# Three 256-column matmuls per weight tile, into one PSUM accumulator, in a two-layer encoder trunk

## The chip, the cores and the metric

The kernel runs on one core of a Trainium2 chip. The time is device time in microseconds, the median of several executions. The engines are named as in the profile: PE is TensorE (PEld its loads of stationary tiles), DVE is VectorE, ACT is ScalarE, POOL is GpSimd, SP the engine that issues most DMAs.

## The reference

An encoder trunk of two layers, 256 tokens of 2048 features, all in float32:

```python
for i in range(DEPTH):                       # DEPTH = 2
    a = rms_norm(h, mix_norm[i])
    if i % N_MIXERS == 0:
        mixed = neighborhood_attention(a, na_w_qkv[j], na_rpb[j], na_w_o[j])   # layer 0
    elif i % N_MIXERS == 1:
        mixed = short_conv_mixer(a, sc_w_in[j], sc_conv_w[j], sc_w_out[j])     # layer 1
    h = h + mixed
    h = h + conv_glu_ffn(rms_norm(h, ffn_norm[i]), ffn_w_up[i], ffn_conv_w[i],
                         ffn_conv_b[i], ffn_w_down[i])
return rms_norm(h, final_norm)
```

Almost all of the work is in the products with the weights: 2048 x 6144 and 2048 x 2048 in each mixer, 2048 x 11264 and 5632 x 2048 in each gated MLP.

## The kernel before

Everything is kept transposed: features on the 128 partitions, the 256 tokens on the free axis. A weight tile of 128 x 128 is stationary, the activations of one feature tile move. float32 is carried in two parts of the type float32r: a weight w as wh + wl, an input x as xh + xl. Of the four products three are taken, wh*xh + wh*xl + wl*xh. An input tile (`a`, `act`) holds xh in its columns 0 to 255 and xl in 256 to 511.

The **weight stream** is two lists made ahead: `chunks`, the weights in order of first use (8 tiles of 128 x 128 as a rule, 512 KB), and `items`, TensorE's work. `prep_to` keeps the preparation four chunks ahead: a DMA on SP's queue to `raw` (L94), a copy by ACT to `hi` (L95), a subtraction by DVE to `lo` (L96). `Phase` makes the items of one product: an output tile of 128 features is a sum over `nk` weight tiles (16, or 22 for the second product of the MLP). `Phase.run` issues the matmuls, L134 and L135 for each weight tile. L134 multiplies wh with all 512 columns, xh and xl side by side, into a full PSUM bank: wh*xh lands in the lower half, wh*xl in the upper. L135 multiplies wl with xh, 256 columns, and adds into the upper half. So the lower half holds the main product, the upper the corrections. Four such accumulators (`mm`) are in turn.

When an output tile is complete, its **evacuation** adds the halves. After products that take a norm's input, `normed` copies the upper half to SBUF (L176, ACT), adds the lower (L177, DVE) and multiplies by the norm's factor rstd (L178, DVE). After products that end a branch, `residual` adds both halves to the stream hT (L211, L212, DVE). Then follow the convolutions, the gate, the next input's split in two parts, or the squares for the next norm (POOL, L219 and L220).

The **order** around it: layer 0 is queries and keys with the scores of two heads (`scores`, L265 to L267) and the values with the mix (`Values`, L328 to L330, and `mix`, L302 to L304) spread between the items by `after`, then the product with wo, then the MLP in two halves. Layer 1 is the product with wsc, the short convolution, the product with wscout, the MLP. At the start the inputs arrive while the first three output tiles are computed in turns over four weight tiles; their evacuation waits until rstd is known (`first_stats`: L205 sums the squares, L194 to L199 make rstd, L457 brings it to the other layout). Engines take their instructions in order; a scheduler fixes that order when the program is built, and it may place a small matmul such as L205 between the matmuls of other items.

`scores` and `mix` have products in three parts as well, each as three matmuls of 256 columns into one place:

```python
nc.tensor.matmul(o[:, i, :], lhsT=vh, rhs=p[:, :S], start=k == 0, stop=False)
nc.tensor.matmul(o[:, i, :], lhsT=vh, rhs=p[:, S:], start=False, stop=False)
nc.tensor.matmul(o[:, i, :], lhsT=vl, rhs=p[:, :S], start=False, stop=k == 1)
```

Of the kernel before, what the change touches and what calls it, by code (L numbers as in the profile page):

```python
"""Two-layer hybrid encoder trunk, kept transposed on chip: features on partitions, tokens on the
free axis. Weight tiles are stationary. A float32 product is carried by float32r parts:
w = wh + wl and x = xh + xl exactly, with 12 significant bits each, and
w*x = wh*xh + (wh*xl + wl*xh) to float32's rounding, so three passes give what four would.
"""
# [7 lines left out]
F32 = mybir.dt.float32  # L13
# [6 lines left out]
P = 128  # L20
D = 2048
S = 256
# [6 lines left out]
EPS = 1e-6  # L29
# [4 lines left out]

# columns of the packed parameters
C_NORM = 0
# [9 lines left out]
def trunk(ctx, tc, xT, par, bias, wqk, wv, wo, wsc, wscout, wup, wdown, out):  # L46
    nc = tc.nc
# [8 lines left out]
    hT = cp.tile([P, KT, S], F32, name="hT")  # L56
# [12 lines left out]
    nc.scalar.dma_start(out=pt[:, :C_SC], in_=par[:, :C_SC])  # L69
    # the activation table and TensorE's clock, while the first loads are under way  # L70
    nc.scalar.copy(out=tp.tile([P, 1], F32, name="m", tag="m"), in_=ones[:, :1])
# [10 lines left out]

# [1 line left out]
    items = []      # PE work, in order  # L84
    chunks = []     # weights, in order of first use
    prepped = []
# [12 lines left out]
    class Phase:  # L99
        """fts output tiles, each a sum over nk tiles of src, ended by evac(ft, psum)."""  # L100

# [24 lines left out]
        def run(self, ft, c, k0, ka, kb):  # L126
            hi, lo = prepped[c]
            if ka == 0:
                self.ps[ft] = pm.tile([P, 2 * S], F32, name="mm", tag="mm")
            ps = self.ps[ft]  # L130
            for k in range(ka, kb):
                x = self.src[k]
                o = (k - k0) * P
                nc.tensor.matmul(ps, lhsT=hi[:, o:o + P], rhs=x, start=k == 0, stop=False)  # L134
                nc.tensor.matmul(ps[:, S:], lhsT=lo[:, o:o + P], rhs=x[:, :S], start=False,  # L135
                                 stop=k == self.nk - 1)
            if kb == self.nk:
                held.append((self, ft))
                if not waiting:
                    evacuate()  # L140
# [7 lines left out]

    later = []      # (item number, function)

# [4 lines left out]

# [1 line left out]
    def split(dst, src):  # L157
        """src (float32) into its two float32r parts."""
        nc.scalar.copy(out=dst[:, :S], in_=src)
        nc.vector.tensor_sub(out=dst[:, S:], in0=src, in1=dst[:, :S].bitcast(F32))  # L160
# [12 lines left out]
    def normed(dst, ps):  # L173
        """dst = (both parts of a product of un-normalised input) * rstd."""
        corr = tp.tile([P, S], F32, name="corr", tag="corr", bufs=3)
        nc.scalar.copy(out=corr, in_=ps[:, S:])  # L176
        nc.vector.tensor_add(out=corr, in0=ps[:, :S], in1=corr)  # L177
        nc.vector.tensor_mul(out=dst, in0=corr, in1=rstd)  # L178

    def conv(x, w, b):  # L180
        """Centred three-tap convolution along the tokens of a zero-padded tile."""
        c = tp.tile([P, S], F32, name="conv", tag="conv", bufs=4)
        if b is None:
            nc.scalar.activation(c, x[:, 1:S + 1], AF.Copy, scale=w[1])
        else:
            nc.scalar.activation(c, x[:, 1:S + 1], AF.Identity, scale=w[1], bias=b)  # L186
        for tap in (0, 2):
            nc.vector.scalar_tensor_tensor(out=c, in0=x[:, tap:tap + S], scalar=w[tap], in1=c,  # L188
                                           op0=ALU.mult, op1=ALU.add)
        return c  # L190

    def rsqrt(dst, v, r, t, sums):
        """dst = (sums / D + EPS) ** -0.5, with a Newton step after the table's square root."""
        nc.vector.tensor_scalar(out=v, in0=sums, scalar1=1.0 / D, scalar2=EPS, op0=ALU.mult, op1=ALU.add)  # L194
        nc.scalar.activation(r, v, AF.Sqrt)
        nc.vector.reciprocal(out=r, in_=r)
        nc.vector.tensor_mul(out=t, in0=r, in1=r)
        nc.vector.scalar_tensor_tensor(out=t, in0=t, scalar=-0.5, in1=v, op0=ALU.mult, op1=ALU.mult)
        nc.vector.scalar_tensor_tensor(out=dst, in0=t, scalar=1.5, in1=r, op0=ALU.add, op1=ALU.mult)  # L199

    def stats(sums):
        """rstd of every token, on all partitions, from sums of squares."""
        ps = pa.tile([P, S], F32, name="st", tag="st")
        for i, x in enumerate(sums):
            nc.tensor.matmul(ps, lhsT=ones, rhs=x, start=i == 0, stop=i == len(sums) - 1)  # L205
        v = tp.tile([P, S], F32, name="v", tag="v", bufs=1)
        rt = tp.tile([P, 2, S], F32, name="rt", tag="s")
        rsqrt(rstd, v, rt[:, 0, :], rt[:, 1, :], ps)

    def residual(ps, ft):  # L210
        nc.vector.tensor_add(out=hT[:, ft, :], in0=ps[:, S:], in1=hT[:, ft, :])  # L211
        nc.vector.tensor_add(out=hT[:, ft, :], in0=ps[:, :S], in1=hT[:, ft, :])  # L212

# [8 lines left out]
    def to_norm(n, a):  # L222
        """Evacuation of a branch's output: residual, squares, and the next norm's input."""
        def evac(ft, ps):
            residual(ps, ft)
            a[ft] = a_tile()
            scaled_split(a[ft], hT[:, ft, :], norm_g(n, ft))
            squares(ft)
            if ft == KT - 1:
                after(1, lambda: stats([acc]))  # L230
        return evac

# [1 line left out]
    a0 = [None] * KT  # L234
# [49 lines left out]
    def probs(h):  # L284
        """The probabilities with keys on partitions: per key tile, both parts of (128, 256 queries)."""
        x = heads[h]
        tr = pa.tile([P, 2, S], F32, name="tr", tag="tr")
        for k in range(2):
            for t in range(2):
                nc.tensor.transpose(tr[:, k, t * P:(t + 1) * P], x["p"][:, t, k * P:(k + 1) * P], ident)  # L290
        x["pT"] = [act_tile(), act_tile()]
        for k in range(2):
            split(x["pT"][k], tr[:, k, :])

    def mix(hs, v):
        """Two heads' values, weighted by their probabilities."""
        o = pa.tile([P, 2, S], F32, name="o", tag="o")
        for i, h in enumerate(hs):
            for k in range(2):
                p = heads[h]["pT"][k]  # L300
                vh, vl = (x[:, h % 4 * P:(h % 4 + 1) * P] for x in v[k])
# [3 lines that stand above are left out]
        for i, h in enumerate(hs):  # L305
            oT[h] = act_tile()
            split(oT[h], o[:, i, :])
            heads[h].clear()

    class Values:  # L310
        """The values of four heads, tokens on partitions: the input is stationary."""

# [30 lines left out]

# [1 line left out]
    yT = [None] * KT  # L345
# [18 lines left out]

# [1 line left out]
    glu = {}  # L366
# [22 lines left out]

# [1 line left out]
    def last_evac(ft, ps):  # L391
        residual(ps, ft)
        if ft < KT - 1:
            squares(ft)
            nc.scalar.activation(hT[:, ft, :], hT[:, ft, :], AF.Copy, scale=norm_g(4, ft))
            if ft == 0:
                # brings in the table that the last norm needs
                nc.scalar.activation(tp.tile([P, 1], F32, name="m", tag="m"), ones[:, :1], AF.Sqrt)
            return
        q = tp.tile([P, S], F32, name="q", tag="q")  # L400
        nc.vector.tensor_mul(out=q, in0=hT[:, ft, :], in1=hT[:, ft, :])
        nc.vector.tensor_scalar_mul(hT[:, ft, :], hT[:, ft, :], norm_g(4, ft))
        # rstd with tokens on partitions, then spread over the partitions by a product with a diagonal
        col = pa.tile([P, 2], F32, name="o", tag="o")
# [30 lines left out]

# [1 line left out]
    sq = []  # L437
# [37 lines left out]
def _tiles(w, cols):  # L475
    """(K, N) -> (tiles of 128 columns in the order of cols, 128 rows of a K tile, K tiles * 128)."""
    import numpy as np
    k, n = w.shape
    t = np.asarray(w).reshape(k // P, P, n // P, P).transpose(2, 1, 0, 3)
    return np.ascontiguousarray(t[cols]).reshape(len(cols), P, k)  # L480
# [61 lines left out]
```

## Time and profile before

| | |
|---|---|
| median of 3 runs | 2264.58 us (2258.64 to 2269.03) |
| span of the profiled execution | 2279.6 us |
| PE busy | 2256.4 us, 99%, 12716 matmuls and as many loads |
| DVE busy | 1638.7 us, 72% |
| ACT busy | 1148.1 us, 50% |
| POOL busy | 178.1 us, 8% |
| DMA | 421.10 MB, mean 185 GB/s |
| mean granted TensorE clock | 0.994 of full speed |

The profiled execution has only its span as its own time; it is 15.0 us over the median of the runs. A group's line has the source line, the engine, the operation, output and inputs by the program's names, the shape of out and in, the count, then busy time, the mean of one in ns, and the engine's idle time just ahead with what ended most of it. Durations of matmuls overlap, since the engine is a pipeline: the distance between two starts says what one costs. Counts of matmuls on the profile can be above the program's where a float32 product takes two passes.

### The profile page before, as it was taken

What the parts mean: (1) busy time and instruction counts of PE and PEld (TensorE: products, weight loads), DVE (VectorE), ACT (ScalarE), POOL (GpSimd) and SP (SyncE); (2) the same over time, 40 slices, a digit from 0 to 9 for tenths busy, and PEclk for the clock granted to TensorE, in tenths of its full rate; (3) what the DMA queues carried; (4) which work ended last, traced back from release to release, by engine and by line L of the source; (5) the groups of instructions that cost most, each with busy time, mean ns of one, the idle gap of its engine ahead of it and who ended that gap; (6) DMA issues with size and microseconds to landing.
All of it is one profiled execution on the core that took longest, in us unless ns stands there. A gap on an engine that the chain in (4) does not pass through costs nothing.

```text
span 2279.6 us, 33316 instructions
## 1 busy us (share of the span) xinstructions
PE 2256.4 (99%) x12716; PEld 1955.2 (86%) x12716; DVE 1638.7 (72%) x2408; ACT 1148.1 (50%) x1694; POOL 178.1 (8%) x174
## 2 busy tenths in 40 slices
PE   8999999999999999999999999999999999999997
PEld 7888888888888888888888888888888888888886
DVE  8777668877775577776676666777777557777754
ACT  6555554555543455554444444455555334555542
POOL 3011003100000000001210000330000000000021
PEclk8999999999999999999999999999999999999998
DMA  7565555555556655556655555555555665555563
GB/s 241 189 187 177 178 173 191 183 187 187 187 175 189 193 189 188 186 181 182 189 188 185 186 188 188 186 185 185 186 186 183 181 190 192 186 187 187 175 189 104
DMA packets 119841, 421.10 MB, mean 185 GB/s; under 512 B 13568, under 2 KB 13568, under 8 KB 119680
## 3 DMA queue, kind: packets, MB, share of 16 engines
q1 hardware_dynamic: 117936, 414.72, 57.0%
q0 software_dynamic: 1024, 3.15, 0.5%
q8 instruction: 100, 1.64, 0.3%
q10 hardware_dynamic: 720, 1.09, 0.1%
q14 instruction: 61, 0.50, 0.1%
HBM read 416.81 MB, written 2.10 MB: 184 GB/s over the span
## 4 chain that ended last, share of the span: by engine, by line
PE 97%; DVE 1%; issue 0%; DMA 0%; POOL 0%; ACT 0%; SPq 0%; DVEq 0%; ACTq 0%
PE mm L134 61%; PE mm L135 31%; PE mm L328 1%; PE mm L329 1%; PE mm L330 1%; DMA hT<-in_xT 0%; DVE lo L96 0%; PE tr L290 0%; DVE hT L416 0%; PE st L205 0%; POOL acc L220 0%; PE o L302 0%; PE o L304 0%; PE o L303 0%; PE sc L266 0%
## 5 line engine op out<-in xcount | busy, mean ns | idle before, releaser
L134 PE MATMUL mm<-a,hi 128*128 128x512 f32 x4096 | 1454.4, 400 | 1.8 <-ACT hi L95 1.4
L96 DVE TENSOR_TENSOR lo<-raw,hi 128x1024 fp32r<-128x1024 f32 (+2 forms) x806 | 979.1, 1215 | 544.2 <-ACT hi L95 540.6
L95 ACT CAST hi<-raw 128x1024 fp32r<-128x1024 f32 (+2 forms) x806 | 827.2, 1027 | 1012.6 <-issue 599.2
L135 PE MATMUL mm<-a,lo 128*128 128x256 f32 x4096 | 1153.5, 282 | 5.2 <-DVE lo L96 5.2
L134 PEld LDWEIGHTS mm<-a,hi 128*128 128x128 f32 x4096 | 771.7, 188 | 193.1 <-ACT hi L95 1.7
L135 PEld LDWEIGHTS mm<-a,lo 128*128 128x128 f32 x4096 | 775.6, 189 | 7.3 <-DVE lo L96 6.9
L134 PE MATMUL mm<-act,hi 128*128 128x512 f32 x1920 | 675.6, 397 | 0.0
L135 PE MATMUL mm<-act,lo 128*128 128x256 f32 x1920 | 537.9, 280 | 0.0
L134 PEld LDWEIGHTS mm<-act,hi 128*128 128x128 f32 x1920 | 360.4, 188 | 87.9 <-DVE act L160 0.3
L135 PEld LDWEIGHTS mm<-act,lo 128*128 128x128 f32 x1920 | 362.4, 189 | 0.1
L188 DVE SCALAR_TENSOR_TENSOR conv<-pad,pt,conv 128x256 f32<-128x256 f32 x384 | 185.1, 482 | 11.1 <-ACT conv L186 4.3
L216 POOL TENSOR_TENSOR acc<-hT 128x256 f32<-128x256 f32 x4 | 3.4, 853 | 1599.2 <-DVE hT L212 1599.2
L186 ACT ACTIVATE conv<-pad,pt 128x256 f32<-128x256 f32 x176 | 105.2, 598 | 6.9 <-DVE pad L178 6.9
L177 DVE TENSOR_TENSOR corr<-mm,corr 128x256 f32<-128x256 f32 x256 | 106.8, 417 | 1.0 <-ACT corr L176 0.8
L176 ACT COPY corr<-mm 128x256 f32<-128x256 f32 x256 | 92.9, 363 | 0.9 <-PE mm L135 0.8
L219 POOL TENSOR_TENSOR q<-hT 128x256 f32<-128x256 f32 x59 | 70.6, 1196 | 242.1 <-DVE hT L212 242.1
L178 DVE TENSOR_TENSOR pad<-corr,rstd 128x256 f32<-128x256 f32 x176 | 75.1, 427 | 5.9
L211 DVE TENSOR_TENSOR hT<-mm,hT 128x256 f32<-128x256 f32 x96 | 40.2, 422 | 30.1 <-PE mm L135 30.0
L220 POOL TENSOR_TENSOR acc<-acc,q 128x256 f32<-128x256 f32 x59 | 59.8, 1014 | 4.6
L164 DVE SCALAR_TENSOR_TENSOR a<-hT,pt,a 128x256 fp32r<-128x256 f32 x64 | 55.5, 878 | 4.8 <-ACT a L163 4.8
L328 PE MATMUL mm<-hi,a 128*128 128x512 f32 x128 | 50.7, 396 | 0.0
L329 PE MATMUL mm<-lo,a 128*128 128x512 f32 x128 | 49.9, 390 | 0.0
(95 smaller groups left out, 762.0 us busy)
## 6 DMA issues: line engine op xcount, KB each, us to landing
raw<-in_wup SPq DMA_DIRECT2D x352, 512.0 KB, 3.7
raw<-in_wdown SPq DMA_DIRECT2D x128, 512.0 KB, 3.7
raw<-in_wsc SPq DMA_DIRECT2D x96, 512.0 KB, 3.6
raw<-in_wqk SPq DMA_DIRECT2D x58, 512.0 KB, 3.7
raw<-in_wdown SPq DMA_DIRECT2D x64, 384.0 KB, 3.2
raw<-in_wv SPq DMA_DIRECT2D x32, 512.0 KB, 3.8
raw<-in_wo SPq DMA_DIRECT2D x32, 512.0 KB, 3.6
raw<-in_wscout SPq DMA_DIRECT2D x32, 512.0 KB, 3.6
```

The costliest lines, as they stand in the source:

```text
L95: nc.scalar.copy(out=hi[:, :w], in_=raw[:, :w])
L96: nc.vector.tensor_sub(out=lo[:, :w], in0=raw[:, :w], in1=hi[:, :w].bitcast(F32))
L134: nc.tensor.matmul(ps, lhsT=hi[:, o:o + P], rhs=x, start=k == 0, stop=False)
L135: nc.tensor.matmul(ps[:, S:], lhsT=lo[:, o:o + P], rhs=x[:, :S], start=False, stop=k == self.nk - 1)
L176: nc.scalar.copy(out=corr, in_=ps[:, S:])
L177: nc.vector.tensor_add(out=corr, in0=ps[:, :S], in1=corr)
L178: nc.vector.tensor_mul(out=dst, in0=corr, in1=rstd)
L186: nc.scalar.activation(c, x[:, 1:S + 1], AF.Identity, scale=w[1], bias=b)
L188: nc.vector.scalar_tensor_tensor(out=c, in0=x[:, tap:tap + S], scalar=w[tap], in1=c, op0=ALU.mult, op1=ALU.add)
L219: nc.gpsimd.tensor_mul(out=q, in0=hT[:, ft, :], in1=hT[:, ft, :])
L328: nc.tensor.matmul(self.ps[t], lhsT=xh, rhs=wh, start=k == 0, stop=False)
L329: nc.tensor.matmul(self.ps[t], lhsT=xh, rhs=wl, start=False, stop=False)
```

## The change

The accumulator of an output tile becomes 256 columns, half a bank. For each weight tile there are three matmuls of 256 columns, all into it: wh with xh, wh with xl, wl with xh. `normed` is one multiplication from PSUM, `residual` one addition.

```diff
         def run(self, ft, c, k0, ka, kb):
             hi, lo = prepped[c]
             if ka == 0:
-                self.ps[ft] = pm.tile([P, 2 * S], F32, name="mm", tag="mm")
+                self.ps[ft] = pm.tile([P, S], F32, name="mm", tag="mm")
             ps = self.ps[ft]
             for k in range(ka, kb):
                 x = self.src[k]
-                o = (k - k0) * P
-                nc.tensor.matmul(ps, lhsT=hi[:, o:o + P], rhs=x, start=k == 0, stop=False)
-                nc.tensor.matmul(ps[:, S:], lhsT=lo[:, o:o + P], rhs=x[:, :S], start=False,
-                                 stop=k == self.nk - 1)
+                wh, wl = (w[:, (k - k0) * P:(k - k0 + 1) * P] for w in (hi, lo))
+                nc.tensor.matmul(ps, lhsT=wh, rhs=x[:, :S], start=k == 0, stop=False)
+                nc.tensor.matmul(ps, lhsT=wh, rhs=x[:, S:], start=False, stop=False)
+                nc.tensor.matmul(ps, lhsT=wl, rhs=x[:, :S], start=False, stop=k == self.nk - 1)
...
     def normed(dst, ps):
-        corr = tp.tile([P, S], F32, name="corr", tag="corr", bufs=3)
-        nc.scalar.copy(out=corr, in_=ps[:, S:])
-        nc.vector.tensor_add(out=corr, in0=ps[:, :S], in1=corr)
-        nc.vector.tensor_mul(out=dst, in0=corr, in1=rstd)
+        nc.vector.tensor_mul(out=dst, in0=ps, in1=rstd)
...
     def residual(ps, ft):
-        nc.vector.tensor_add(out=hT[:, ft, :], in0=ps[:, S:], in1=hT[:, ft, :])
-        nc.vector.tensor_add(out=hT[:, ft, :], in0=ps[:, :S], in1=hT[:, ft, :])
+        nc.vector.tensor_add(out=hT[:, ft, :], in0=ps, in1=hT[:, ft, :])
```

Lines below `Phase.run` have other numbers after the change: the three matmuls are L134, L135 and L136, the multiplication of `normed` is L175, the addition of `residual` L208, the statistics L202, the product that brings rstd to the other layout L453.

The order of instructions on TensorE, in the first up product of layer 0, at the boundary between two output tiles (numbers tell one buffer from the next; `mm` is the accumulator, `a` an input tile, `hi` and `lo` the parts of a weight chunk). Before:

```order
L134 MATMUL mm_8720<-a_4021,hi_8626 128x512
L135 MATMUL mm_8720<-a_4021,lo_8627 128x256
L134 MATMUL mm_8720<-a_4074,hi_8626 128x512
L135 MATMUL mm_8720<-a_4074,lo_8627 128x256
L134 MATMUL mm_8775<-a_3318,hi_8658 128x512
L135 MATMUL mm_8775<-a_3318,lo_8659 128x256
```

and with the change:

```order
L134 MATMUL mm_10544<-a_4730,hi_10432 128x256
L135 MATMUL mm_10544<-a_4730,hi_10432 128x256
L136 MATMUL mm_10544<-a_4730,lo_10433 128x256
L134 MATMUL mm_10612<-a_3761,hi_10469 128x256
L135 MATMUL mm_10612<-a_3761,hi_10469 128x256
L136 MATMUL mm_10612<-a_3761,lo_10470 128x256
```

Each pair has become three; nothing else stands between them. On DVE at the same output tile, the evacuation between the splits of weights, before:

```order
L177 TENSOR_TENSOR corr_8759<-mm_8720,corr_8759 128x256
L178 TENSOR_TENSOR pad0_78<-corr_8759,rstd_76 128x256
L96 TENSOR_TENSOR lo_8828<-raw_8826,hi_8827 128x1024
L188 SCALAR_TENSOR_TENSOR conv_8763<-pad0_78,pt_73,conv_8763 128x256 x2
L96 TENSOR_TENSOR lo_8851<-raw_8849,hi_8850 128x1024
L177 TENSOR_TENSOR corr_8814<-mm_8775,corr_8814 128x256
```

and with the change:

```order
L175 TENSOR_TENSOR pad0_78<-mm_10544,rstd_76 128x256
L96 TENSOR_TENSOR lo_10639<-raw_10637,hi_10638 128x1024
L185 SCALAR_TENSOR_TENSOR conv_10600<-pad0_78,pt_73,conv_10600 128x256 x2
L96 TENSOR_TENSOR lo_10678<-raw_10676,hi_10677 128x1024
L175 TENSOR_TENSOR pad1_79<-mm_10612,rstd_76 128x256
```

The addition to `corr` is gone, the rest of the order is kept. At the start of the program, on TensorE, the place of the last two of the four statistics matmuls (`st`) among the first three output tiles (`mm_226`, `mm_235`, `mm_244`), before:

```order
L134 MATMUL mm_235<-a_184,hi_218 128x512
L135 MATMUL mm_235<-a_184,lo_219 128x256
L205 MATMUL st_376<-act_178,ones_75 128x256
L134 MATMUL mm_244<-a_166,hi_262 128x512
L205 MATMUL st_376<-act_178,ones_75 128x256
L135 MATMUL mm_244<-a_166,lo_263 128x256
```

and with the change, where the last one comes behind the whole of the third tile (`mm_252`), and the product with rstd behind the whole of the fourth (`mm_468`):

```order
L135 MATMUL mm_252<-a_214,hi_332 128x256
L136 MATMUL mm_252<-a_214,lo_333 128x256
L202 MATMUL st_424<-act_178,ones_75 128x256
L134 MATMUL mm_468<-a_103,hi_350 128x256
...
L136 MATMUL mm_468<-a_214,lo_369 128x256
L453 MATMUL st_437<-pt_73,rstd_76 128x1 x2
L134 MATMUL mm_552<-a_103,hi_386 128x256
```

The last statistics matmul has moved some 15 weight tiles later, the product with rstd some 6.

## The prediction

> **What bounds the kernel now.** I read the page first (busy shares, the chain that ended last, the groups), then the waits of TensorE alone, then stretches of the span, then single rows in order of time.
>
> ```profile
> span 2279.6 us, 33316 instructions
> PE 2256.4 (99%) x12716; PEld 1955.2 (86%) x12716; DVE 1638.7 (72%) x2408; ACT 1148.1 (50%) x1694; POOL 178.1 (8%) x174
> PE 97%; DVE 1%; issue 0%; DMA 0%; POOL 0%; ACT 0%; SPq 0%; DVEq 0%; ACTq 0%
> L134 PE MATMUL mm<-a,hi 128*128 128x512 f32 x4096 | 1454.4, 400 | 1.8 <-ACT hi L95 1.4
> L134 PE MATMUL mm<-act,hi 128*128 128x512 f32 x1920 | 675.6, 397 | 0.0
> L177 DVE TENSOR_TENSOR corr<-mm,corr 128x256 f32<-128x256 f32 x256 | 106.8, 417 | 1.0 <-ACT corr L176 0.8
> L176 ACT COPY corr<-mm 128x256 f32<-128x256 f32 x256 | 92.9, 363 | 0.9 <-PE mm L135 0.8
> L211 DVE TENSOR_TENSOR hT<-mm,hT 128x256 f32<-128x256 f32 x96 | 40.2, 422 | 30.1 <-PE mm L135 30.0
> q8 instruction: 100, 1.64, 0.3%
> ```
>
> TensorE is 97% of the chain and idle for 2279.6 - 2256.4 = 23.2 us. There are 4096 + 1920 = 6016 weight tiles, each one pair of matmuls, so 1 ns on a weight tile is 6.0 us on the end. Nothing else here has such a lever. Its waits (total, times, longest) are small and lie at the start, at the four norms and at the end:
>
> ```profile
> PE mm L135 <- DVE lo L96: 5.2, 4, 2.3
> PE st L205 <- POOL acc L220: 2.0, 3, 0.9
> ```
>
> So the question is what a pair costs in the stream, from start to start, and not the 400 and 280 ns that the rows give as durations, which overlap. The L134 matmuls alone, by stretches (the second number of PE is how many touch the stretch):
>
> ```profile
> 324.80:398.00 73.20, 73.20 (x212) 39.49 (x212) 1.00 0.55 180
> 414.00:800.00 386.00, 386.00 (x1094) 205.34 (x1093) 1.00 0.59 186
> 1434.50:1517.00 82.50, 82.42 (x239) 44.62 (x239) 1.00 0.58 191
> 1523.00:1900.00 377.00, 377.00 (x1068) 200.49 (x1067) 1.00 0.59 186
> 1900.00:2257.00 357.00, 357.00 (x1011) 189.80 (x1011) 1.00 0.56 177
> ```
>
> A matmul that began up to 0.4 us ahead is counted too, so a pair takes (386.0 + 0.4) / 1094 = 353 ns; the three long stretches together give 1121.2 / 3173 = 353.4 ns. The two stretches that are the products with wo and wscout give (73.6 + 82.9) / 451 = 347.0 ns, at the same granted clock of 1.00. So one form of work runs at two paces. With 512 pairs at 347.0 and 5504 at 353.4 the mean is **352.9 ns**.
>
> **The change part by part.** Per weight tile the 512-column matmul becomes two of 256 columns with the same stationary tile, and the 256-column one stays. The columns streamed stay 768. The loads of stationary tiles go from two to three, if the second product loads again. That form, three 256-column matmuls adding into one place, the first two with one stationary tile, already runs in this kernel: the scores (L265 to L267) and the mix of values (L302 to L304). Here are the pair, and four such bursts by their first and last starts, each with the matmul that follows it:
>
> ```profile
> 999.82 0.28 PE L135 MATMUL mm<-a,lo 128*128 128x256 f32 x1
> 999.93 0.40 PE L134 MATMUL mm<-a,hi 128*128 128x512 f32 x1
> 1000.16 0.28 PE L135 MATMUL mm<-a,lo 128*128 128x256 f32 x1
> 1000.28 0.40 PE L134 MATMUL mm<-a,hi 128*128 128x512 f32 x1
> 1000.52 0.28 PE L135 MATMUL mm<-a,lo 128*128 128x256 f32 x1
> 1000.64 0.40 PE L134 MATMUL mm<-a,hi 128*128 128x512 f32 x1
> ...
> 95.88 0.28 PE L302 MATMUL o<-act,vh 128*128 128x256 f32 x1
> 97.30 0.40 PE L134 MATMUL mm<-a,hi 128*128 128x512 f32 x1
> ...
> 100.08 0.28 PE L302 MATMUL o<-act,vh 128*128 128x256 f32 x1
> 101.50 0.40 PE L134 MATMUL mm<-a,hi 128*128 128x512 f32 x1
> ...
> 137.72 0.28 PE L265 MATMUL sc<-qk,qk 128*128 128x256 f32 x1
> 138.44 0.39 PE L134 MATMUL mm<-a,hi 128*128 128x512 f32 x1
> ...
> 323.32 0.28 PE L303 MATMUL o<-act,vh 128*128 128x256 f32 x1
> 324.65 0.28 PE L135 MATMUL mm<-act,lo 128*128 128x256 f32 x1
> ```
>
> Twelve matmuls take 1.42 us in each of the first two bursts (118.3 ns each), six take 0.72 us in the third (120.0), and eleven take 1.33 us in the last (120.9), which follows a short stall of TensorE. All 41 together: 4.89 / 41 = 119.3 ns; without the last burst 3.56 / 30 = 118.7 ns. A 512-column matmul beside it in the stream is 0.23 to 0.24 us (999.93 to 1000.16, 1000.28 to 1000.52), so two halves at 118 to 120 replace it at about its price. The term is the small rest.
>
> I take 118.9 ns, between the two means and nearer to the unstalled bursts, since the new stream is as unbroken as they are: a weight tile costs 356.7 ns, +3.8 ns against 352.9, and 6016 x 3.8 = **+23 us**. Bounds: at 120.9 it is 362.7 ns, +59 us. Below, the three 256-column slots of L135 in the rows above (0.11, 0.12, 0.12) give 350 ns for three, -17 us.
>
> The Trainium skill, "TensorE: Matmul & The Clock Gate", section "Back-to-back issue gap", gives N / 2.4 + 2.5 ns for a warm matmul of N columns: 215.8 + 109.2 = 325.0 ns for the pair and 327.5 for three, so by it the split costs one more fixed 2.5 ns, an estimate of +15 us. The trace does not agree with its absolute size (353.4 against 325.0), but its sign is that of the bursts.
>
> **The evacuation.** normed loses the ACT copy (256 x 363 ns = 93 us of ACT) and one DVE add (256 x 417 = 107 us); residual loses one of its two DVE adds (96 x 422 = 40 us). They lie beside TensorE's stream: the chain gives DVE 1% and ACT 0%, and TensorE waits only in the places listed above. They count where the last tile of a stage is waited for: the three norms, where the statistics wait on POOL's sum, which waits on the residual, and the end.
>
> ```profile
> 408.51 0.42 DVE L211 TENSOR_TENSOR hT<-mm,hT 128x256 f32<-128x256 f32 x1 [0.54 <-PE mm L135]
> 408.97 0.42 DVE L212 TENSOR_TENSOR hT<-mm,hT 128x256 f32<-128x256 f32 x1
> ```
>
> One step of 0.46 us goes in each: 4 x 0.46 = **-1.8 us**. The 2.0 us of waits on POOL above bear three of them. If the cover were to fail, with DVE or ACT late with a weight tile's parts, it would show as waits on lo and hi, which this part makes rarer and not more frequent. Without it the most that a lighter DVE could return is the 5.2 us of waits on lo.
>
> **The start.** The order of instructions moves there. The last of the four statistics matmuls stood 51 instructions of TensorE ahead of the product with rstd (L457), some 25 pairs or 25 x 353 = 8.8 us of work; now it stands after all three first tiles, 48 matmuls ahead, 16 weight tiles or 5.7 us. The chain between them runs through DVE:
>
> ```profile
> 30.73 0.59 PE L205 MATMUL st<-act,ones 128*128 128x256 f32 x2
> ...
> 39.99 0.50 PE L457 MATMUL st<-pt,rstd 128*128 128x1 f32 x4
> ```
>
> From 30.73 to 39.99 it took 9.3 us. DVE's order keeps as many splits of weights between its steps, and one corr add of 0.42 goes from among them: 8.8 us. Late next is TensorE's product with rstd and behind it, in order, the whole stream: 8.8 - 5.7 = **+3 us**. Bounds: 0 if the chain shortens by more than I count, since less work competes, and +5 if the scores behind it wait for the split of q and k as well.
>
> **Instructions.** 6016 matmuls and as many loads more. Their code was 1.64 MB for 2 x 12716 instructions at 0.3% of the DMA engines, so it becomes 1.64 x 18732 / 12716 = 2.4 MB at under 0.5%. I cost it at nothing: 100 packets over the span are one in 23 us, then one in 15 us, and they come beside the stream of matmuls. Were each packet late, TensorE would show idle time in the long stretches, which have none now.
>
> **Sum** against the profiled execution: 2279.6 + 23 - 1.8 + 3 = 2303.8 us of span. That execution lies 15.0 us over the median of the runs shown (2264.58, 2258.64 to 2269.03), which I take as the same on both sides: **2288.8 us**.
>
> **Rivals.** Under 0.5% (11 us) a measurement here can't tell from no change.
>
> *The bursts were fed, the stream is not.* If 118 ns holds only while TensorE has its next loads lined up, the unbroken stream runs at the pace of the burst behind the stall, 120 to 120.9 ns, and decides as soon as the three loads and three matmuls of a weight tile can't be prepared in 356 ns. Then +43 to +59 us: 2308 to 2325. For it: that burst, and the third one, at 120.0. Against: 24 matmuls in two bursts of twelve show no slowing. The Trainium skill, the same page, section "Wait — 56ns, not 53.3ns?", tells of some 62 ns of sequencer time for each matmul where hardware decoding is off; by it alone, taken for loads too, six instructions would be 372 ns, an estimate of 2381 us. The bursts at 118.3 for two instructions speak against that.
>
> *The pace falls into the faster rhythm.* The pair shows two paces, 353.4 and 347.0 ns, at one clock, so the pace isn't fixed by form alone, and a stream of one uniform size could settle at the 350 ns of the L135 slots: 6016 x -2.9 = -17, with -1.8 and no loss at the start 2245 to 2249: **faster**. It decides once a 256-column matmul stays under 117 ns. Against: none of the four bursts is under 118.
>
> *Nothing measurable.* Each matmul at 117.0 to 118.2 ns gives 351.0 to 354.6 ns, -11 to +10 us, with +1.2 for the ends: 2255 to 2276. For it: the columns are the same 768, and 118.2 lies just under the long bursts. Against: so do few of the rows.
>
> *The second load is not made.* Then a weight tile would have two loads as before. The mix has the very form and loads each time:
>
> ```profile
> L303 PEld LDWEIGHTS o<-act,vh x32: 187/188/189, 95.9 to 324.3; 128*128 128x128 f32 x32
> ```
>
> So I give it no chance of its own; its time would lie within the case of nothing measurable.
>
> **How the numbers follow.** Forecast 0.52 (118.3 to 119.9 ns, 2278 to 2307), the unfed stream 0.23, nothing measurable 0.16, the faster rhythm 0.09. Slower by over 0.5% is the first two, 0.75; within 0.5% 0.16; faster 0.09. The range 2264 to 2316 leaves out the faster rhythm and the upper half of the unfed stream.
>
> **What would show it.** Of the profile after: 18048 rows of 256-column matmuls on the three lines, with starts 118.9 ns apart in the long stretches (1.07 us for nine); if 120 or more, the unfed stream; if 117 or less, the faster rhythm. No corr rows, DVE near 1490 us and ACT near 1055, with no waits of TensorE added in the stream. At the start, TensorE idle for about 3 us ahead of the product with rstd. The prediction is wrong if the stream keeps 353 ns per weight tile, or if idle time of TensorE between weight tiles appears that these rows don't have.

## The result, and the profile after

| | before | changed |
|---|---|---|
| median | 2264.93 us (2258.64 to 2269.03) | **2328.92 us** (2327.04 to 2329.04) |
| ratio | | **1.0281** (95% interval 1.0238 to 1.0324) |
| span of the profiled execution | 2279.6 us | 2327.2 us |

The changed kernel is 2.8% slower. The forecast had the sign and the place right and the size wrong: 2288.8 us, in a range of 2264 to 2316.

The page of the changed kernel: span, engines, chain by engine and by line, then the groups that answer to those shown of before.

```profile
span 2327.2 us, 44561 instructions
PE 2302.9 (99%) x18732; PEld 2282.7 (98%) x18732; DVE 1516.6 (65%) x2056; ACT 1078.4 (46%) x1438; POOL 172.9 (7%) x174
PE 97%; DVE 1%; DMA 1%; issue 0%; ACT 0%; POOL 0%; SPq 0%; DVEq 0%; ACTq 0%
...
L136 PE MATMUL mm<-a,lo 128*128 128x256 f32 x4096 | 1163.1, 284 | 5.5 <-DVE lo L96 5.5
L134 PE MATMUL mm<-a,hi 128*128 128x256 f32 x4096 | 1163.7, 284 | 2.6 <-ACT hi L95 1.7
L135 PE MATMUL mm<-a,hi 128*128 128x256 f32 x4096 | 1161.9, 284 | 0.3 <-DVE a L164 0.3
...
L175 DVE TENSOR_TENSOR pad<-mm,rstd 128x256 f32<-128x256 f32 x176 | 75.0, 426 | 85.0 <-PE mm L136 84.9
```

TensorE carries 97% of the chain as before. The loads of stationary tiles (PEld) rose from 86% to 98% of the span: there are three per weight tile, and one is under way at nearly every moment. DVE fell by 122 us and ACT by 70, and nothing of it came back: DVE's multiplication now waits 85 us for TensorE. TensorE's idle time is 2327.2 - 2302.9 = 24.3 us, against 23.2. So the loss is not in waits but in the pace of the stream. Starts in the middle of it, and the L135 matmuls of two stretches (one per weight tile):

```profile
999.74 0.28 PE L135 MATMUL mm<-a,hi 128*128 128x256 f32 x1
999.86 0.28 PE L136 MATMUL mm<-a,lo 128*128 128x256 f32 x1
999.98 0.28 PE L134 MATMUL mm<-a,hi 128*128 128x256 f32 x1
...
1000.46 0.28 PE L135 MATMUL mm<-a,hi 128*128 128x256 f32 x1
```

```profile
600.00:800.00 200.00, 157.19 (x557) 106.74 (x556) 1.00 0.62 182
1800.00:2000.00 200.00, 157.19 (x557) 106.72 (x556) 1.00 0.62 185
```

Six matmuls take 0.72 us, 120.0 ns each; a weight tile takes 200.28 / 557 = 360 ns, in every stretch alike. Against the 352.9 of the first profile that is 6016 x 7.1 = 42.7 of the 47.6 us between the two spans.

### The profile page after: what moved, and what is told of

Same layout as the page of the kernel before. It is cut to its first block, busy times and chain, and to the rows that moved or that the text cites. A ratio compares the mean times of both kernels' runs of the same rounds, so it can differ in the third digit from the quotient of the medians.

```text
span 2327.2 us, 44561 instructions
## 1 busy us (share of the span) xinstructions
PE 2302.9 (99%) x18732; PEld 2282.7 (98%) x18732; DVE 1516.6 (65%) x2056; ACT 1078.4 (46%) x1438; POOL 172.9 (7%) x174
## 3 DMA queue, kind: packets, MB, share of 16 engines
q8 instruction: 146, 2.39, 0.4%
## 4 chain that ended last, share of the span: by engine, by line
PE 97%; DVE 1%; DMA 1%; issue 0%; ACT 0%; POOL 0%; SPq 0%; DVEq 0%; ACTq 0%
PE mm L134 31%; PE mm L135 31%; PE mm L136 31%; PE mm L324 1%; PE mm L325 1%; PE mm L326 1%; DVE lo L96 0%; DMA raw<-in_wqk 0%; PE tr L286 0%; DVE a L164 0%; DMA hT<-in_xT 0%; POOL acc L216 0%; DVE hT L412 0%; ACT hi L95 0%; PE o L298 0%
## 5 line engine op out<-in xcount | busy, mean ns | idle before, releaser
L136 PE MATMUL mm<-a,lo 128*128 128x256 f32 x4096 | 1163.1, 284 | 5.5 <-DVE lo L96 5.5
L134 PE MATMUL mm<-a,hi 128*128 128x256 f32 x4096 | 1163.7, 284 | 2.6 <-ACT hi L95 1.7
L135 PE MATMUL mm<-a,hi 128*128 128x256 f32 x4096 | 1161.9, 284 | 0.3 <-DVE a L164 0.3
L136 PEld LDWEIGHTS mm<-a,lo 128*128 128x128 f32 x4096 | 788.8, 193 | 6.9 <-DVE lo L96 6.7
L134 PEld LDWEIGHTS mm<-a,hi 128*128 128x128 f32 x4096 | 789.0, 193 | 3.3 <-ACT hi L95 2.0
L135 PEld LDWEIGHTS mm<-a,hi 128*128 128x128 f32 x4096 | 789.1, 193 | 0.8 <-DVE a L164 0.6
L135 PE MATMUL mm<-act,hi 128*128 128x256 f32 x1920 | 543.4, 283 | 0.0
L134 PE MATMUL mm<-act,hi 128*128 128x256 f32 x1920 | 543.4, 283 | 0.0
L136 PE MATMUL mm<-act,lo 128*128 128x256 f32 x1920 | 543.3, 283 | 0.0
L135 PEld LDWEIGHTS mm<-act,hi 128*128 128x128 f32 x1920 | 368.6, 192 | 0.0
L134 PEld LDWEIGHTS mm<-act,hi 128*128 128x128 f32 x1920 | 368.6, 192 | 0.0
L136 PEld LDWEIGHTS mm<-act,lo 128*128 128x128 f32 x1920 | 368.6, 192 | 0.0
L175 DVE TENSOR_TENSOR pad<-mm,rstd 128x256 f32<-128x256 f32 x176 | 75.0, 426 | 85.0 <-PE mm L136 84.9
L216 POOL TENSOR_TENSOR acc<-acc,q 128x256 f32<-128x256 f32 x59 | 84.5, 1433 | 4.6
L208 DVE TENSOR_TENSOR hT<-mm,hT 128x256 f32<-128x256 f32 x96 | 40.5, 425 | 36.0 <-PE mm L136 34.7
L215 POOL TENSOR_TENSOR q<-hT 128x256 f32<-128x256 f32 x59 | 39.0, 662 | 260.8 <-DVE hT L208 260.8
```

Source lines behind the costliest of these rows:

```text
L134: nc.tensor.matmul(ps, lhsT=wh, rhs=x[:, :S], start=k == 0, stop=False)
L135: nc.tensor.matmul(ps, lhsT=wh, rhs=x[:, S:], start=False, stop=False)
L136: nc.tensor.matmul(ps, lhsT=wl, rhs=x[:, :S], start=False, stop=k == self.nk - 1)
L175: nc.vector.tensor_mul(out=dst, in0=ps, in1=rstd)
L208: nc.vector.tensor_add(out=hT[:, ft, :], in0=ps, in1=hT[:, ft, :])
L215: nc.gpsimd.tensor_mul(out=q, in0=hT[:, ft, :], in1=hT[:, ft, :])
```

## The experiments

They ran on two chips, each beside runs of the kernel before on the same chip.

**The kernel before, profiled again.** No edit.

> The kernel before, unchanged, profiled a second time. Its first profile (2279.6 us) lay 15 us over the median of its runs (2264.9), while the changed kernel's profile and runs agree. Theory of the two paces: a stretch of the pair stream locks into 347.0 or 353.4 ns per weight tile, and which one it gets differs from execution to execution. Then this profile shows the same two paces with another share of them, and its span lies between 2250 and 2280 us, with about 2350 weight tiles more at 347 ns for a span near 2265 (15 us / 6.4 ns). Rival: the first profile lost its 15 us in one place, at the start or in stalls; then all long stretches show 353.4 ns again and the span is 2279 us or the difference stands in idle time of TensorE.

2269.19 us median over 10 runs (2256.53 to 2271.15), ratio 0.9998 (0.9977 to 1.0019). The L134 matmuls of this execution, three stretches:

```profile
900.00:1150.00 250.00, 250.00 (x709) 132.96 (x708) 1.00 0.59 185
1434.50:1500.00 65.50, 65.43 (x185) 34.67 (x186) 1.00 0.57 185
1800.00:2000.00 200.00, 200.00 (x578) 108.19 (x577) 1.00 0.61 193
```

In the first and the last row a pair takes 250.4 / 709 = 353 ns and 200.4 / 578 = 347 ns. In the first profile the stretch from 1900 to 2257 us ran at 353. The same program, at the same granted clock, has another pace in the same place: the whole MLP of layer 1 went at 347 here, 353 there. Its span is 2269.3 us, 10.3 shorter. From 1523 to 2257 us there are some 2100 weight tiles at 6.4 ns each, 13 us, which is the difference to within 3 us; the product with wscout, at 347 in the first profile, had the slow pace here (the middle row) and takes 1.6 us of it back. TensorE's idle time is 24.1 us here and 23.2 there, so the rival of a loss in one place falls and the theory of two paces stands. The profiled execution itself took 2271.15 us, 1.85 over its span; the changed kernel's took 2329.01, 1.8 over its span. So the first profile's execution, by the same margin, took some 2281 us. The 13 runs of the kernel before beside the later experiments, on the other chip, show how far its time varies: five from 2251.4 to 2252.6, one at 2257.1, four from 2264.1 to 2265.7, three from 2283.4 to 2284.8. They stand in groups, as stretches of one pace or the other would make them, and the first profile lies nearest to the slowest. That the paces make the groups is argued and not shown, since none of the 13 was profiled; and on the chip of this profile 27 runs lay between 2255.3 and 2271.2 us, none as slow as the first profile.

**The split alone.** Three matmuls of 256 columns, but the corrections stay in the upper half and the evacuation is that of before:

```diff
-                nc.tensor.matmul(ps, lhsT=hi[:, o:o + P], rhs=x, start=k == 0, stop=False)
+                nc.tensor.matmul(ps[:, :S], lhsT=hi[:, o:o + P], rhs=x[:, :S], start=k == 0, stop=False)
+                nc.tensor.matmul(ps[:, S:], lhsT=hi[:, o:o + P], rhs=x[:, S:], start=False, stop=False)
```

> The split alone: three 256-column matmuls per weight tile, but the second and third still add into the separate upper half, and the evacuation is that of before (ACT copy, two DVE additions). If the whole loss is the pace of the 256-column matmuls, the stream runs at 360 ns per weight tile and the time is that of the changed kernel plus about 2 us for the longer evacuations (2326 to 2334). If adding three times into one place of PSUM is what costs, the pace falls to 347 to 357 ns and the time to 2250 to 2310.

2323.64 us, ratio 1.0250 (1.0229 to 1.0271). Its stream (L135, one stretch) is that of the changed kernel:

```profile
600.00:800.00 200.00, 157.19 (x557) 106.74 (x556) 1.00 0.62 183
```

So it is the split, not the adding into one place, that costs. This kernel has the heavy evacuation and is still 5 us faster than the changed one, which was not expected: its time was to lie at 2326 or over. The 5 us are at the start, in one of its waits and in the stretch from 40 to 60 us:

```profile
PE st L458 <- DVE rstd L200: 1.1, 1, 1.1
...
40.00:60.00 20.00, 18.86 (x159) 18.66 (x158) 19.50 (x40) 15.39 (x29) 3.54 (x3) 1.00 0.75 231
```

The changed kernel waited 3.5 us for rstd, had a granted clock of 0.83 in that stretch and got 109 matmuls through it where this one has 159 (its rows are shown with the last experiment): 50 x 120 ns are 6 us. What the light evacuation did return is seen in the waits of TensorE, first of this kernel, then of the changed one:

```profile
PE st L206 <- POOL acc L221: 1.7, 3, 0.8
PE o L408 <- DVE q L402: 1.4, 1, 1.4
```

```profile
PE o L403 <- DVE q L397: 0.9, 1, 0.9
```

The wait for POOL's sum at the norms, 1.7 us in all, is no more among the waits of the changed kernel, and the one at the end is 0.5 us shorter: 2.2 us.

**Half the moving columns, half the stationary columns, half of both.** The changed kernel with smaller matmuls, to tell a load that sets the pace from a fixed cost of a matmul or of its issue. With `n` 128 instead of 256 columns, or `m` 64 instead of 128, or both, in all but the first and last weight tile of a sum:

```diff
-                nc.tensor.matmul(ps, lhsT=wh, rhs=x[:, :S], start=k == 0, stop=False)
+                nc.tensor.matmul(ps[:m, :n], lhsT=wh[:, :m], rhs=x[:, :n], start=k == 0, stop=False)
```

(and the same in the other two).

> The changed kernel with the moving operand halved to 128 columns in all but the first and last weight tile of an output tile (half the tokens are left out of those sums). Theory of the load: each matmul needs a load of its own and the load with its handover sets the pace; then the matmuls stay at 107 to 120 ns. Theory of the columns: 256 columns at the clock plus a fixed 13 ns make the 120; then 128 columns give 53 + 13 = 67 ns and bursts of three at 200 ns. Theory of the issue: two instructions per matmul at 60 ns each; 120 ns as before. Other engines or DMA may set the total time if TensorE becomes fast.

> The changed kernel with the stationary tile halved to 64 columns in all but the first and last weight tile of an output tile (half the output features are left out of those sums); the moving operand stays 256 columns. With 128 moving columns the pace stayed at 112 ns, so the load of 128 columns has a floor of about 112 ns. Theory of load and stream together: 120 ns is the stream of 256 columns (107) and a handover of 13 that the load of 128 columns makes necessary; with a load of 64 columns the load is done early and the pace falls to 107 to 114. Theory of a fixed cost per matmul: the 13 ns stay whatever is loaded, 120 ns. Theory of the issue: 120 ns.

> The changed kernel with both halved, 64 stationary and 128 moving columns, in all but the first and last weight tile of an output tile (half of the features and half of the tokens are left out of those sums). Theory of the load: its floor halves, and within a chunk the matmuls follow at 55 to 75 ns. Theory of the issue (two instructions per matmul set the floor of 112 ns): 110 to 120 ns. The total time will then be set by the preparation of the weights, so the pace is read inside bursts.

Rows of the three kernels in order, each within a chunk, first start and a later one:

```profile
999.74 0.27 PE L136 MATMUL mm<-a,hi 128*128 128x128 f32 x1
...
1000.41 0.28 PE L136 MATMUL mm<-a,hi 128*128 128x128 f32 x1
```

```profile
999.77 0.28 PE L135 MATMUL mm<-a,hi 128*64 128x256 f32 x1
...
1000.45 0.28 PE L135 MATMUL mm<-a,hi 128*64 128x256 f32 x1
```

```profile
999.80 0.22 PE L135 MATMUL mm<-a,hi 128*64 128x128 f32 x1
...
1000.10 0.22 PE L137 MATMUL mm<-a,lo 128*64 128x128 f32 x1
```

From the first start to the later one there are six, six and five matmuls: 0.67 / 6 = 112 ns, 0.68 / 6 = 113 ns, 0.30 / 5 = 60 ns. (Over some 500 steps within chunks of each trace, where TensorE doesn't wait, the means are 111, 113.5 and 60.)

| ns per matmul | 256 moving columns | 128 moving columns |
|---|---|---|
| 128 stationary columns | 120 | 112 |
| 64 stationary columns | 113 | 60 |

(Times of the whole: 2202.5, 2227.7 and 1825.0 us, one run each; in the last TensorE waits for the preparation of weights, 123.0 us for lo and 96.6 for hi.) Issue is out: the same two instructions per matmul go through in 60 ns. What the columns alone take is seen in the changed kernel where the granted clock is half (the engines' table of 49 to 54 us, and two of its rows with five matmuls from start to start):

```profile
49.00:54.00 5.00, 5.00 (x23) 5.00 (x24) 4.05 (x10) 1.34 (x4) 0.00 (x0) 0.50 0.83 270
...
51.04 0.41 PE L136 MATMUL mm<-a,lo 128*128 128x256 f32 x1
52.11 0.41 PE L263 MATMUL sc<-qk,qk 128*128 128x256 f32 x1
```

1.07 / 5 = 214 ns at 0.50 is 107 ns at full clock for 256 columns, 53 for 128 and 214 for 512. So the changed stream pays 13 ns over its columns for each matmul. With a fixed 13 ns and nothing else, 128 moving columns would have taken 67 ns, and they took 112: the 128 stationary columns hold the pace there, since with 64 of them it is 60. So 128 stationary columns, and their load as the likely cause, set a floor of some 112 ns. But that floor lies under 120 and is not what the changed kernel runs at. The 13 ns are also there where a load is much shorter than the stream, in the values of the kernel before, whose 512-column matmuls follow each other, each with a load of its own (18 of them from the first row to the second):

```profile
78.97 0.39 PE L328 MATMUL mm<-hi,a 128*128 128x512 f32 x1
...
83.05 0.39 PE L328 MATMUL mm<-hi,a 128*128 128x512 f32 x1
```

4.08 / 18 = 227 ns, again 13 over the 214 of the columns; and 227 - 120 = 107 ns for 256 columns more is the figure of the half clock once again. With 64 stationary columns the 13 become 6: 113 over 107 (and 60 over 53, where a load may hold it too). So each matmul with its load pays 13 ns with 128 stationary columns, for 256 moving columns as for 512, and about half of that with half the stationary columns. Whether the handover from one load to the next takes them, or the rows of output, which were halved with it, isn't shown apart.

The sum over a weight tile comes out: 3 x 107 + 2 x 13 = 347 ns is the fast pace of the pair, 3 x 107 + 3 x 13 = 360 is the changed kernel. The third load with its matmul is what the change pays, 13 ns. Against the slow pace of 353 ns, which held most of the first profile, only 7 of them show.

The Trainium skill, "TensorE: Matmul & The Clock Gate", section "LDWEIGHTS (loading the stationary operand)", gives a load as its columns / 1.2 ns: 106.7 for 128, 53.3 for 64. The paces with 128 moving columns, 112 and 60, are 5 to 7 ns over these and agree. The Trainium skill, the same page, section "Back-to-back issue gap", says that spacing in a real stream is set by load and matmul together, which the table bears out; its isolated figure of N / 2.4 + 2.5, 109.2 ns for 256 columns, does not hold here (120, and 113 with the shorter load).

**All 512-column matmuls of a chunk first.** The kernel before, in another order:

```diff
             for k in range(ka, kb):
-                x = self.src[k]
                 o = (k - k0) * P
-                nc.tensor.matmul(ps, lhsT=hi[:, o:o + P], rhs=x, start=k == 0, stop=False)
-                nc.tensor.matmul(ps[:, S:], lhsT=lo[:, o:o + P], rhs=x[:, :S], start=False,
+                nc.tensor.matmul(ps, lhsT=hi[:, o:o + P], rhs=self.src[k], start=k == 0, stop=False)
+            for k in range(ka, kb):
+                o = (k - k0) * P
+                nc.tensor.matmul(ps[:, S:], lhsT=lo[:, o:o + P], rhs=self.src[k][:, :S], start=False,
                                  stop=k == self.nk - 1)
```

> The kernel before with one thing changed: within a chunk of 8 weight tiles all 512-column matmuls come first, then all 256-column ones. Same matmuls, same loads, same accumulator. In the traces 512-column matmuls in a row (values) go at 227 ns each and 256-column ones in a row at 120.0. If the slow pace of the pair (353.4) comes from the alternation of the two lengths, this stream runs at 227 + 120 = 347 ns everywhere, 5504 x 6.4 = 35 us less than the first profile: a span of 2240 to 2250, and 2240 to 2255 in time. If the pace is set by the mean load on the load path, it stays at 347 to 353 in a varying share: 2258 to 2280.

2260.51 us (2258.89 to 2263.47), ratio 0.9974 (0.9958 to 0.9990). The time is that of the second expectation, but the pace is neither: it lies between, and does not vary. One stretch of the 512-column matmuls, and rows of eight matmuls each:

```profile
430.00:1100.00 670.00, 482.10 (x1921) 344.70 (x1919) 1.00 0.59 188
...
1001.24 1.12 PE L136 MATMUL mm<-a,lo 128*128 128x256 f32 x8
1002.19 2.00 PE L133 MATMUL mm<-a,hi 128*128 128x512 f32 x8
1004.03 1.11 PE L136 MATMUL mm<-a,lo 128*128 128x256 f32 x8
```

Eight of 512 columns take 1.84 us, 230 ns each, where 227 was expected from the values' rows above; eight of 256 take 0.95, 118.8 each and not 120. Going over to 512 columns costs some 0.03 us, going over to 256 returns 0.01. The pace is 670.4 / 1921 = 349 ns, and 349 to 350 in every stretch, and the runs lie within 4.6 us of each other, where those of before spread over 14.6 (2256.5 to 2271.2).

**Half as many changes of length.** As above, and every second chunk of an output tile begins with its 256-column matmuls:

```diff
+            parts = [0, 1] if k0 // CH % 2 == 0 else [1, 0]
+            for part in parts:
```

> As hi_then_lo, but every second chunk of an output tile begins with the 256-column matmuls, so there are half as many changes of length. In hi_then_lo each row of eight began with about 20 ns more than 8 x (227 + 120), and then settled. If the change of length is what costs, the mean falls from 349.2 to 348 ns per weight tile: 6016 x 1.2 = 7 us under hi_then_lo, 2250 to 2257. If the slow first matmuls belong to each chunk, whatever its order, the time stays at 2258 to 2264.

2254.23 us (2252.86 to 2254.88, ten runs), ratio 0.9954 (0.9912 to 0.9997). The 512-column matmuls of two stretches:

```profile
400.00:1100.00 700.00, 483.23 (x2012) 368.77 (x2012) 1.00 0.59 188
1600.00:2200.00 600.00, 414.34 (x1722) 315.45 (x1722) 1.00 0.60 189
```

700.4 / 2012 = 348.1 and 600.4 / 1722 = 348.7 ns. That is the pace of the first expectation, under the 349 above, and the time has fallen too (by 6 us, on another chip): the change of length costs, and not the beginning of a chunk. This kernel has the lowest median of those tried, 0.5% under before, with an interval that nearly reaches 1, since the runs of before vary: their five fastest, 2251.4 to 2252.6, are as fast as this one always is, the others slower. So it is the steadier kernel, and a gain over the best runs isn't shown.

**The statistics earlier.** The changed kernel with `after(9, first_stats)` in place of `after(11, first_stats)`.

> The changed kernel with the statistics of the first norm issued two items earlier, so that the last statistics matmul stands 8 weight tiles earlier and the product with rstd 2. In the changed kernel TensorE waited 3.5 us there, and its clock was at half speed for 6.8 us around it. If that place is what the start costs, the wait falls under 1.5 us and the time by 2 to 6 us, to 2323 to 2327. If the half-speed stretch comes whatever the wait, or the wait moves to the scores behind it, the time stays at 2327 to 2330.

2322.10 us (2321.25 to 2322.17), ratio 1.0241 (1.0164 to 1.0318), against 2327.04 to 2329.04 for the changed kernel: 6.8 us less, a little more than expected. TensorE at the place, first in the changed kernel (two rows of its timeline, and the engines' table of the stretch from 40 to 60 us), then in this one:

```profile
47.35 0.73 PE L453 MATMUL st<-pt,rstd 128*128 128x1 f32 x4 [3.49 <-DVE rstd L196]
48.98 0.55 PE L134 MATMUL mm<-a,hi 128*128 128x256 f32 x1 [0.90 <-DVE qk L175]
...
40.00:60.00 20.00, 15.61 (x109) 15.35 (x108) 16.18 (x29) 11.90 (x19) 1.60 (x2) 0.83 0.70 214
```

```profile
42.15 0.61 PE L453 MATMUL st<-pt,rstd 128*128 128x1 f32 x4
...
40.00:60.00 20.00, 19.29 (x157) 18.67 (x156) 19.66 (x38) 14.11 (x25) 3.10 (x4) 1.00 0.82 264
```

The wait of 3.5 us is gone, the one of 0.9 behind it is 0.2, and the granted clock of the stretch is 1.00 where it was 0.83: 0.17 x 20 = 3.4 us of TensorE's time. 3.5 + 0.7 + 3.4 = 7.6 us is the estimate from these; by count the stretch has 157 matmuls in place of 109, 48 x 120 ns = 5.8 us, and from 22 to 40 us it is 128 in place of 120, another 1.0 us, which makes the 6.8. That the wait brought the clock down isn't shown apart: both went together.

## Why the prediction was wrong

Forecast 2288.8, measured 2328.9, 40.1 us apart. By its own steps:

- **The pace of the three matmuls** (the step "I take 118.9 ns"): 120.0 in place of 118.9, 6016 x (360 - 356.7) = **20 us**. The mechanism (columns equal, the third load as the price) was right, the term was mis-sized: the third load costs 13 ns, seen as 7 against the pace that the first profile mostly had, where 3.8 were forecast. A mean over four short bursts was taken for a stream's pace. The two bursts of twelve took 1.42 us, 0.02 less than 12 x 120; why isn't shown, but the 256-column matmuls behind a row of 512-column ones come early in the experiment above too (eight in 0.95 us and not 0.96). The burst that read 120.9 had one slot that was 0.04 us longer, which the prediction called a stall, and it was given as a rival at 0.23 ("the bursts were fed, the stream is not"). The rival's number was right and its reason wrong: issue doesn't limit.
- **The offset of 15.0 us** between profile and median (the step "which I take as the same on both sides"): the changed kernel's median is 1.7 us over its span, so this step failed by **16.7 us**. With 1.7 over the span in place of 15.0 under it the forecast is 2305.5. The range, to 2316, had no place for such an error. The offset was not the profiler's. That execution had the slow pace in nearly the whole of its stream, as the table of stretches showed, and its own time, by the margin of 1.8 us, was some 2281 us. The runs around the median were faster; that they had more of the fast pace, as the second profile did, is the likely reason, though they weren't profiled. Two paces were named in the prediction, and yet their share was taken as the same in the profile and in the runs.
- **The start**: +3 us forecast; the wait came, 3.5 us at the place named, with the clock at half speed for a part of it, which the step left out. Issuing the statistics earlier returned 6.8 us, 3.8 more than the step had. **3.5 us** are left for it and for all the rest when the two terms above are taken off.
- **The evacuation**: -1.8 us forecast. Against the kernel with the split alone, the waits at the norms and the end are 2.2 us shorter, where the step put them. In the time it doesn't show, since the start lost more. DVE and ACT came to 1516.6 and 1078.4 us, 27 and 23 over the forecast's 1490 and 1055, which cost no time.
- **Instructions**: 2.39 MB at 0.4%, no idle time in the stream: as forecast. The second load was made, as forecast: 18732 loads.
- **The faster rhythm** (0.09) and **nothing measurable** (0.16) did not come: a stream of one length has one pace here, 120.

With the rival's 2308.5 for 120 ns, plus 16.7 and 3.5, one is at 2328.7. That sum has to close, since the 3.5 is what was left over; the 20 and the 16.7 are measured.

## What to carry to other kernels

A matmul with 128 stationary columns paid 13 ns here over the columns that it streamed, 120 for 107 and 227 for 214, so the wider the moving operand, the less of it goes to that price. Splitting a wide matmul to simplify what follows it pays the price once more for each weight tile, 6016 times here; the lighter evacuation, off the critical path, returned 2.2 us of waits. And before a sum is moved from a profile to the median of the runs, ask whether the profiled execution is a typical one: the distance between its span and its own time (1.8 us here) is known, and the rest is the kernel's own variation.

## What the runs showed of the hardware that I had not expected

The alternation of 512- and 256-column matmuls has two paces, 347 and 353.4 ns per pair, at a granted clock of 1.00, and which one a stretch of 700 us holds differs from execution to execution. Over all 6016 weight tiles the 6.4 ns between them are 39 us, enough for the 33 us between the fastest and the slowest run of the kernel before, but only two of its executions were profiled. The fast pace is what its two matmuls cost in rows of their own, 227 and 120 ns. Rows of one length hold one pace each, and in rows of eight a change of length there and back costs some 0.02 us; in the alternation, where every matmul changes it, a pair pays between nothing and 6 ns for it. What decides which pace the alternation falls into is open: in the long stretches of the first two profiles the pace changed only where TensorE was interrupted, at the norms and the ends of stages, but no run here chose it. The order with half as many changes runs at 348 to 349 ns in both stretches shown and takes 2252.9 to 2254.9 us in ten runs.
